# Hybrid attention and RWKV-7 layer on one core: more steps between transfers and their users, follow-ups of dense tiles later, both directions of a scan step together

## The chip, the cores and the metric

The kernel runs on one core of a Trainium2 chip, in float32 throughout. The metric is the device time of one launch in microseconds (us), lower is better. Time is given as the median of the runs; a profiled execution has a time of its own, against which its trace is read.

## The reference, cut to what matters

One layer over 1024 tokens of width 1024. One projection feeds two groups of heads; their outputs are projected back and added to x, then an MLP follows.

```python
h = _rms_norm(x, ln1_g[layer])
proj = h @ w_in[layer]                       # 3*512 columns for q, k, v; 1792 more for u
attn = _dilated_window_attention(q, k, v, q_norm_g[layer], k_norm_g[layer])
rwkv = _rwkv7_bidirectional(u, ...)
x = x + jnp.concatenate([attn, rwkv], axis=-1) @ w_out[layer]
h = _rms_norm(x, ln2_g[layer])
x = x + jnp.square(jax.nn.relu(h @ w_up[layer])) @ w_down[layer]
```

Attention has 8 heads of 64 with normalised queries and keys and three dilated windows, whose results are mixed by their softmax sums. The recurrent group has 8 heads as well. Its state is a 64x64 matrix for each head, carried over the tokens once forwards and once backwards:

```python
def step(state, inp):
    r_t, w_t, k_t, v_t, kk_t, a_t = inp
    s_kk = jnp.einsum('bhvk,bhk->bhv', state, kk_t)
    state = (state * w_t[:, :, None, :]
             - s_kk[..., None] * (kk_t * a_t)[:, :, None, :]
             + v_t[..., None] * k_t[:, :, None, :])
    return state, jnp.einsum('bhvk,bhk->bhv', state, r_t)
```

The outputs of both directions are added, normalised for each head, and a bonus term and a gate follow.

## The kernel before, in words

**Layout and order.** Activations lie transposed, channels on the 128 partitions and tokens along the row, in halves (hf) of 512 tokens. A product of two float32 operands is made from three matmuls of split operands (mm3, lines 104 to 107: high by high, low by high, high by low). The program is written in one order, and a scheduler places the instructions of each engine by readiness and by a priority, which is the place in the program; `ahead(n)` lowers the number for a block, so that it goes n places earlier. An engine then runs its own list strictly in order.

**Stages.** A prologue to 52 us loads x and norms it. `in_proj` (line 164) follows to 603 us, `mixers` (line 839) to 987, and `tail` (line 984), with the output projection and the MLP, to the end.

**in_proj** does two things side by side. The generator `dense` (line 353) makes 26 tiles of 128 projected columns: first the 14 tiles of u, then queries, keys and values (tiles 0 to 11). It yields after every few matmuls. Beside it goes the recurrent preparation of the four head pairs p. `per_half` (line 416) normalises keys and builds decays for one half. `unit_a` (line 447) builds for one half and direction the matrices of 8 chunks of 64 tokens: products psg (L496), masked copies G (L501), and the store gd (L504). Then come transposes psb (L508), their copies BK (L512) and stores to rec_dr. `pair_b` (line 520) inverts 16x16 blocks for both halves of a direction: it loads MP from gd (L524), runs 15 vector steps (stmp L534, Tt L536), stores td and loads the block inverses t16 and t16t. `unit_c` (line 556) then widens them to 64x64 with products psd (L564) and vector steps Nb, Yt, TF (L570, L576, L579). `bonus` (line 582) makes the bonus term. `drive(g, rate)` (line 386) advances such a generator; each of its yields gives the dense work `rate` steps, 0.7, and the pairs waiting in the list `back` 0.6 steps (`behind`). When the units are through, a drain loop gives four dense steps for each step of `back`.

**Follow-ups of dense tiles.** A query or key half is evacuated from PSUM as qc (L322) and squared as qsq (L324). Then, at once, `head_inv` (L124 to L128) takes head sums on TensorE (psq) and their reciprocal rn. `head_rep` widens rn to rx on ScalarE (L133) and turns it by four transposes (L136). The half is scaled (L326), split into qhi (L329) and qlo (L331), and both are stored (L332, L333). A value half is evacuated as vc (L342), turned by four transposes (L345), copied as vn (L348) and stored (L350). qsq, qhi and vn share one buffer (tag qt), and qc, rx and qlo have one each. A second set of these buffers exists from `mixers` on.

**mixers** runs the scan: 16 steps of 64 tokens for each direction d. `load` (line 852) fetches one step's matrices, 1152 KB of rec and four pieces of 64 KB for pv and uv. `step` (line 864) is a chain. It starts with products psc with the state pv (L870), a copy B (L872), and products with B (L874). Two copies follow into uv, one on ScalarE (L875) and one on VectorE (L876). Then come products with uv (L879) and the new state (L882, L883). The outputs psY are made from pv (L886) and uv (L888). The two directions are called one after the other under `ahead(400)`; after each pair `fill(20, 4.7)` gives the remaining dense steps, then pieces of attention under `ahead(200)`. Attention has 64 pieces, 8 for each head, about 12 matmul rows of the built order each: scores ps_s (L701, L702), transposes ps_pt (L719), products with the values pv and pvb (L748). From step 8 on, `post` (line 890) finishes a block of 128 tokens of the recurrent output.

## Time and profile before

| | us |
|---|---|
| runs | 1781.92, 1796.67, 1788.32 |
| median | 1788.32 |
| profiled execution | 1784.77 |
| its span | 1783.0 |
| PE busy in the span | 1649.5 (93%) |
| mean granted clock of TensorE | 0.949 |

Engines are PE (TensorE matmul), PEld (its weight load), DVE (VectorE), ACT (ScalarE), POOL (GpSimd) and SP (SyncE, which issues most DMAs). A row of a timeline is start, duration, engine, line, operation, output<-inputs, and in brackets the idle time ahead of it with what ended it. A row of a table of windows gives for each engine busy time and count, then the granted clock as a share of full speed, the mean busy share of the 16 DMA engines and GB/s. A row of waits is engine, group, what released it, total, number and longest.

### The profile page before, as it was taken

The numbers are of one execution on the slowest core, as the hardware profiler recorded it, in microseconds if no ns is written. First come the engines' busy times: TensorE is split into PE (matmuls) and PEld (weight loads), VectorE is DVE, ScalarE is ACT, GpSimd is POOL, SyncE is SP. The second block draws the span as 40 slices with busy tenths as digits, with TensorE's granted clock in tenths as the row PEclk, the third lists the DMA queues.
The fourth block names the chain that finished last, engine by engine and source line by source line (L and its number), as shares of the span: only waits on it lengthen the run. The fifth ranks groups of instructions, "written<-read, shape, count | busy, mean of one in ns | idle before, by whom it ended". The sixth has DMA issues, their size and how long they took to land. (4 is left out here: it accounts for less than half of the span.)

```text
span 1783.0 us, 29922 instructions
## 1 busy us (share of the span) xinstructions
PE 1649.5 (93%) x11912; PEld 1365.7 (77%) x11912; DVE 861.9 (48%) x1754; ACT 543.5 (30%) x990; POOL 294.2 (16%) x322
## 2 busy tenths in 40 slices
PE   7999978979869997989998999999999999999999
PEld 6777767767757776877786887888888888888887
DVE  6655658757545424565775667332332233223321
ACT  5534334443412213535464234211121112112210
POOL 3022112222200000121223115200120012001200
PEclk9999989879879999988998999999999999999999
DMA  6155788878875599997973411111111111111121
GB/s 221 45 142 125 158 160 174 177 176 176 193 173 135 179 223 202 274 272 210 248 198 108 149 48 54 49 53 48 51 50 47 48 48 48 48 48 54 47 96 53
DMA packets 336923, 223.11 MB, mean 125 GB/s; under 512 B 238320, under 2 KB 289408, under 8 KB 332688
## 3 DMA queue, kind: packets, MB, share of 16 engines
q1 hardware_dynamic: 305520, 195.82, 42.7%
q10 hardware_dynamic: 27680, 15.38, 3.2%
q0 software_dynamic: 3584, 10.00, 2.5%
q8 instruction: 94, 1.54, 0.4%
q14 instruction: 45, 0.37, 0.1%
HBM read 150.22 MB, written 70.91 MB: 124 GB/s over the span
## 5 line engine op out<-in xcount | busy, mean ns | idle before, releaser
L101 ACT CAST w3h<-w3raw 128x512 fp32r<-128x512 f32 (+1 forms) x152 | 90.9, 600 | 397.0 <-PE ps L106 387.3
L106 PE MATMUL ps<-h2l,w3h 128*128 128x512 f32 x512 | 199.2, 389 | 1.1 <-DVE h2l L1045 1.1
L105 PE MATMUL ps<-h2h,w3h 128*128 128x512 f32 x512 | 199.3, 390 | 0.7 <-DVE x L1023 0.7
L107 PE MATMUL ps<-h2h,w3l 128*128 128x512 f32 x512 | 199.2, 389 | 0.0
L1089 POOL TENSOR_TENSOR relu<-relu 128x512 f32<-128x512 f32 x64 | 76.8, 1201 | 530.1 <-DVE relu L1088 530.1
L105 PE MATMUL ps_u<-hh,wh 128*128 128x512 f32 x368 | 156.1, 424 | 3.5 <-DVE ur L308 3.5
L107 PE MATMUL ps_u<-hh,wl 128*128 128x512 f32 x368 | 149.6, 407 | 0.0
L106 PE MATMUL ps_u<-hl,wh 128*128 128x512 f32 x368 | 149.3, 406 | 0.0
L102 DVE TENSOR_TENSOR w3l<-w3raw,w3h 128x512 fp32r<-128x512 f32 (+1 forms) x152 | 105.1, 693 | 79.7 <-ACT w3h L101 79.7
L1097 DVE TENSOR_TENSOR x<-x,ps 128x512 f32<-128x512 f32 x64 | 44.0, 688 | 181.7 <-PE ps L107 181.7
L105 PE MATMUL ps<-rw,w3h 128*128 128x512 f32 x320 | 124.7, 390 | 0.9 <-ACT w3h L101 0.9
L105 PE MATMUL ps<-f,w3h 128*128 128x512 f32 x320 | 124.7, 390 | 0.0
L106 PE MATMUL ps<-rw,w3h 128*128 128x512 f32 x320 | 124.5, 389 | 0.0
L107 PE MATMUL ps<-f,w3l 128*128 128x512 f32 x320 | 124.5, 389 | 0.0
L106 PE MATMUL ps<-f,w3h 128*128 128x512 f32 x320 | 124.5, 389 | 0.0
L107 PE MATMUL ps<-rw,w3l 128*128 128x512 f32 x320 | 124.1, 389 | 0.0
L106 PEld LDWEIGHTS ps<-h2l,w3h 128*128 128x128 f32 x512 | 96.1, 188 | 21.3 <-DVE h2l L1045 1.6
L105 PEld LDWEIGHTS ps<-h2h,w3h 128*128 128x128 f32 x512 | 96.1, 188 | 21.0 <-ACT w3h L101 1.1
L107 PEld LDWEIGHTS ps<-h2h,w3l 128*128 128x128 f32 x512 | 96.1, 188 | 19.9
L1088 DVE SCALAR_TENSOR_TENSOR relu<-ps,rep 128x512 f32<-128x512 f32 x64 | 44.1, 691 | 108.4 <-PE ps L107 108.2
L105 PEld LDWEIGHTS ps_u<-hh,wh 128*128 128x128 f32 x368 | 72.0, 196 | 20.2 <-DVE ur L308 4.3
L106 PEld LDWEIGHTS ps_u<-hl,wh 128*128 128x128 f32 x368 | 71.8, 195 | 16.7 <-issue 2.9
(331 smaller groups left out, 3228.7 us busy)
## 6 DMA issues: line engine op xcount, KB each, us to landing
rec<-rec_dr SPq DMA_DIRECT2D x32, 1152.0 KB, 10.0
w3raw<-in_w_up SPq DMA_DIRECT2D x64, 256.0 KB, 2.5
w3raw<-in_w_dn SPq DMA_DIRECT2D x64, 256.0 KB, 2.5
raw<-in_w_in SPq DMA_DIRECT2D x46, 256.0 KB, 2.9
rec_dr<-al POOLq DMA_DIRECT2D x64, 128.0 KB, 4.2
rec_dr<-G SPq DMA_DIRECT2D x32, 256.0 KB, 4.3
rec_dr<-G SPq DMA_DIRECT2D x64, 128.0 KB, 4.4
rec_dr<-BK ACTq DMA_DIRECT2D x16, 512.0 KB, 5.3
```

Source lines behind the costliest of these rows:

```text
L101: nc.scalar.copy(hi, raw)
L102: nc.vector.tensor_sub(lo, raw, r2f(hi))
L105: nc.tensor.matmul(ps, lh, rh, start=start, stop=False)
L106: nc.tensor.matmul(ps, lh, rl, start=False, stop=False)
L107: nc.tensor.matmul(ps, ll, rh, start=False, stop=stop)
L1088: nc.vector.scalar_tensor_tensor(t, pss[hf], 0.0, rep[:, HS[hf]], ALU.max, ALU.mult)
L1089: nc.gpsimd.tensor_mul(t, t, t)
L1097: nc.vector.tensor_add(x1[c][:, HS[hf]], x1[c][:, HS[hf]], ps)
```

## The change

There are five edits. What the program computes stays the same, and so do the counts of PE, POOL and SP work; 32 copies go from ACT to DVE.

1. **Follow-ups later.** A q, k or v half is evacuated (and squared) as before. What follows is put on a list `late`; a new generator `later` around `dense` advances the first entry by one part after each dense yield, and a query or key follow-up has two parts, cut between rx and its transposes (`head_rep` becomes `head_wide` and `head_turn`). qlo now uses the buffer of rx.
2. **Rates.** `drive` gives 0.62 dense steps a yield and 0.8 steps of `back`; the drain loop gives two dense steps for each of `back`.
3. **More yields** in `per_half` (two), in `pair_b` after the MP load (three for one) and after the loads of t16 (three, or one for the second half); the yield of `bonus` goes ahead of its product.
4. **Preparation products earlier.** psg, psb and psd matmuls go under `ahead(150)`; psg and psb get one tile of two PSUM banks instead of two tiles of one, and psg takes head 1 first.
5. **Scan.** `step` does both directions together, under `ahead(2500)` instead of 400. Heads go 1, 0; both uv copies are on DVE, head 1 last; psY takes the product with uv first, then pv.

```diff
@@ qk_tile
-                    rn = head_inv(sq, 1.0 / HD, NORM_EPS, tq, pq)
...
-                    lo = tq.tile([P, 512], F32R, name="qlo")
...
+                    def rest():
+                        rn = head_inv(sq, 1.0 / HD, NORM_EPS, tq, pq)
+                        rx = head_wide(rn, tq)
+                        yield
+                        nc.vector.scalar_tensor_tensor(qc, qc, qg8 if which == 0 else V("kg"), head_turn(rx, pq), ALU.mult,
+                                                       ALU.mult)
...
+                        lo = tq.tile([P, 512], F32R, name="qlo", tag="rx")
...
+                    late.append(rest())
@@ dense
+            def later():
+
+                for _ in dense():
+                    yield
+                    while late and next(late[0], 1) == 1:
+                        late.pop(0)
+                        break
+                while late:
+                    if next(late[0], 1) == 1:
+                        late.pop(0)
+                    yield
+            filler = later()
@@ drive
-                    behind(0.6)
+                    behind(0.8)
@@ unit_a
-                    pss = [pg.tile([P, 4, P], F32, name="psg") for h in range(2)]
-                    for c in range(4):
-                        for h in range(2):
...
+                    pss = pg.tile([P, 2, 4, P], F32, name="psg")
+                    with ahead(150):
+                        for c in range(4):
+                            for h in (1, 0):
...
@@ pair_b
-                yield
+                for _ in range(3):
+                    yield
...
+                    for _ in range(3 - 2 * hf):
+                        yield
                     yield from unit_c(dict(p=p, d=d, cs=slice(hf * 8, hf * 8 + 8), Ab=Ab, t16=t16, t16t=t16t))
@@ in_proj
-                    drive(per_half(w), 0.7)
+                    drive(per_half(w), 0.62)
...
                 behind(1.0)
-                for _ in range(4):
+                for _ in range(2):
                     next(filler, None)
@@ mixers
-        RH = [(r, h) for r in range(4) for h in range(2)]
+        RH = [(r, h) for r in range(4) for h in (1, 0)]
...
-            nc.scalar.copy(uv[H[0], :, H[0]], ps[H[0], 1])
-            nc.vector.tensor_copy(uv[H[1], :, H[1]], ps[H[1], 1])
...
+            for d in range(2):
+                for h in range(2):
+                    nc.vector.tensor_copy(ws[d]["uv"][H[h], :, H[h]], pss[d][H[h], 1])
...
+                for r in range(4):
+                    for h in (1, 0):
+                        nc.tensor.matmul(psY[H[h], d, r], uv[:, r, H[h]], rec[:, r, h * P + 64:h * P + P],
+                                         start=True, stop=False)
+                    for h in (1, 0):
+                        nc.tensor.matmul(psY[H[h], d, r], pv[:, r, H[h]], rec[:, r, 448 + h * 64:512 + h * 64],
+                                         start=False, stop=True)
...
-            for d in range(2):
-                with ahead(400):
-                    step(d, s, ld[s][d], ld[s + 1][d] if s + 1 < NCH else None, psY[:, d])
+            with ahead(2500):
+                step(s, ld[s], ld[s + 1] if s + 1 < NCH else None, psY)
             fill(20, 4.7)
```

Three places of the built order show what this moves. The first is TensorE in the drain after the last preparation unit, around a query or key half. ps_u are its dense products, psd those of the block inverse, psq at L124 the head sums and at L136 (now L139) the transposes. Before:

```order
L107 MATMUL ps_u<-hh_136,wl 128x512
L564 MATMUL psd<-t16t,Nb 64x64 x16
L124 MATMUL psq<-ct,qsq 128x2 x4
L564 MATMUL psd<-Yt,Nb 64x64 x16
L136 MATMUL psq<-ct,rx 128x128 x4
L105 MATMUL ps_u<-hh_129,wh 128x512
```

The same place now:

```order
L107 MATMUL ps_u<-hh_136,wl 128x512
L601 MATMUL psd<-Yt,Nb 64x64 x8
L124 MATMUL psq<-ct,qsq 128x2 x4
L601 MATMUL psd<-Yt,Nb 64x64 x8
L139 MATMUL psq<-ct,rx 128x128 x4
L601 MATMUL psd<-t_5980,Ab 64x64 x16
L601 MATMUL psd<-t16t,Nb 64x64 x16
L124 MATMUL psq<-ct,qsq 128x2 x4
L105 MATMUL ps_u<-hh_129,wh 128x512
...
L107 MATMUL ps_u<-hh_135,wl 128x512
L139 MATMUL psq<-ct,rx 128x128 x4
L105 MATMUL ps_u<-hh_136,wh 128x512
```

The head sums of a half before now stand within the block's products, and between the head sums and the transposes of the next half there are 21 dense products, where before the next product of the block stood.

The second place is VectorE at the seventh of the eight calls of pair_b, from the last masked product G, after which its store and the load of MP go out, to the first stmp, which uses MP. Before:

```order
L501 TENSOR_TENSOR G<-psg,ct 128x512 x2
L475 TENSOR_TENSOR al<-kkn,EE 128x8x64
L326 SCALAR_TENSOR_TENSOR qc<-qc,qg_111,psq 128x512
L331 TENSOR_TENSOR qlo<-qc,qhi 128x512
L576 TENSOR_TENSOR Yt<-psd,t16t 128x512
L481 SCALAR_TENSOR_TENSOR bk<-tm,Ei 128x8x64
L484 TENSOR_TENSOR bk<-kt,Ei 128x8x64
L591 TENSOR_TENSOR us<-pse,us 128x512
L534 TENSOR_TENSOR stmp<-Tt,MP 128x1
```

Now:

```order
L533 TENSOR_TENSOR G<-psg,ct 128x512 x2
L613 TENSOR_TENSOR Yt<-psd,t16t 128x512
L628 TENSOR_TENSOR us<-pse,us 128x512
L506 TENSOR_TENSOR al<-kkn,EE 128x8x64
L127 TENSOR_SCALAR rn<-psq 128x8
L128 RECIPROCAL rn<-rn 128x8
L616 SCALAR_TENSOR_TENSOR TF<-psd,t16t 128x512
L512 SCALAR_TENSOR_TENSOR bk<-tm,Ei 128x8x64
L515 TENSOR_TENSOR bk<-kt,Ei 128x8x64
L334 SCALAR_TENSOR_TENSOR qc<-qc,qg_111,psq 128x512
L568 TENSOR_TENSOR stmp<-Tt,MP 128x1
```

Nine instructions stand between them now, seven before; the follow-up's last step and the block's are others.

The third place is TensorE at a late scan step. psc and psY are the scan's; ps_s, ps_pt, pvb are attention; psb is the finishing of a block. Before:

```order
L748 MATMUL pvb<-vB,ptsb 128x65 x4
L879 MATMUL psc_10078<-uv_9746,rec_9741 64x64 x8
L888 MATMUL psY<-rec_9741,uv_9746 64x64
L886 MATMUL psY<-rec_9741,pv_9743 64x64 x2
L719 MATMUL ps_pt<-ct,sb 128x128 x4
L124 MATMUL psb__9986<-ct,ysq 128x2 x4
L701 MATMUL ps_s<-kk,qh 128x256
L702 MATMUL ps_s<-kk,ql 128x256
```

Now:

```order
L907 MATMUL psc_9934<-pv_9608,rec_9606 64x64 x8
L124 MATMUL psb__9856<-ct,ysq 128x2 x4
L914 MATMUL psc_9934<-B_9952,rec_9606 64x64 x8
L907 MATMUL psc_9935<-pv_9616,rec_9614 64x64
L139 MATMUL psb__9866<-ct,rx 128x128 x4
L907 MATMUL psc_9935<-pv_9616,rec_9614 64x64 x7
L922 MATMUL psc_9934<-uv_9611,rec_9606 64x64 x8
L930 MATMUL psY<-rec_9606,uv_9611 64x64 x2
L933 MATMUL psY<-rec_9606,pv_9608 64x64 x2
```

Where attention stood between the parts of a step, only the other direction and the finishing of a block stand now. Over the whole order 665 of the 760 matmul rows of attention stood ahead of the last psY before, and 307 now; the first of them came after 6 of the 32 direction steps, and now comes after 10.

More of the change, by code (lines that the diff above doesn't have):

```diff
@@ L200, in in_proj @@
                      [pa[0].tile([P, 512], F32, name="ps_u", tag="acc"), pd.tile([P, 512], F32, name="ps_u", tag="psd")],
-                     [pg.tile([P, 512], F32, name="ps_u", tag="psg") for _ in range(2)]]
+                     pg.tile([P, 2, 512], F32, name="ps_u", tag="psg")]
+            early[2] = [early[2][:, hf] for hf in range(2)]
             with tc.tile_pool(name="xp", bufs=2, side="right", reuse_waits="tile") as xp:
@@ L360, in dense @@
                         yield from qk_tile(c % 4, c // 4)
-                    T.setdefault(c - 12, None)
                     yield
@@ L492, in unit_a @@
                 for g in range(2):
[L493 to L497 removed]
+                    pss = pg.tile([P, 2, 4, P], F32, name="psg")
+                    with ahead(150):
+                        for c in range(4):
+                            for h in (1, 0):
+                                nc.tensor.matmul(pss[:, h, c], bk[H[h], 4 * g + c, h:h + 2].rearrange("p a b -> p (a b)"),
+                                                 al[H[h], 4 * g + c].rearrange("p a b -> p (a b)"), start=True, stop=True)
                     yield
@@ L504, in unit_a @@
                     nc.sync.dma_start(mats(gd, h), Gs[h][H[h], :, 0:64])
-                pss = [pg.tile([P, 8, 64], F32, name="psb", tag="psg") for h in range(2)]
-                for c in range(8):
-                    for h in range(2):
-                        nc.tensor.transpose(pss[h][:, c], bk[H[h], c, h:h + 2].rearrange("p a b -> p (a b)"), K("id2")[H[h]])
+                pss = pg.tile([P, 2, 8, 64], F32, name="psb", tag="psg")
+                with ahead(150):
+                    for c in range(8):
+                        for h in range(2):
+                            nc.tensor.transpose(pss[:, h, c], bk[H[h], c, h:h + 2].rearrange("p a b -> p (a b)"), K("id2")[H[h]])
                 yield
@@ L561, in prod @@
                     ps = v3(pd.tile([P, 512], F32, name="psd"))
-                    for c in range(8):
-                        for h in range(2):
-                            nc.tensor.matmul(ps[H[h], c], L[H[h], c], R[H[h], c], start=True, stop=True)
+                    with ahead(150):
+                        for c in range(8):
+                            for h in range(2):
+                                nc.tensor.matmul(ps[H[h], c], L[H[h], c], R[H[h], c], start=True, stop=True)
                     yield
@@ new lines, in mixers, with step @@
+        RH = [(r, h) for r in range(4) for h in (1, 0)]
+        def step(s, ws, wns, psY):
+            cs = [chunk(d, s) for d in range(2)]
+            pss = [pC.tile([P, 2, 4, 64], F32, name=f"psc{d}") for d in range(2)]
+            for d in range(2):
+                for r, h in RH:
+                    nc.tensor.matmul(pss[d][H[h], 0, r], ws[d]["rec"][:, r, h * P:h * P + 64], ws[d]["pv"][:, r, H[h]],
+                                     start=True, stop=True)
+            Bs = [rt.tile([P, 4, 64], F32, name=f"B{d}") for d in range(2)]
+            for d in range(2):
+                nc.scalar.copy(Bs[d], pss[d][:, 0])
+            for d in range(2):
+                for r, h in RH:
+                    nc.tensor.matmul(pss[d][H[h], 1, r], ws[d]["rec"][H[h], r, 384:448], Bs[d][H[h], r], start=True, stop=True)
+            for d in range(2):
+                for h in range(2):
+                    nc.vector.tensor_copy(ws[d]["uv"][H[h], :, H[h]], pss[d][H[h], 1])
+            for d in range(2):
+                rec, uv, pv = (ws[d][n] for n in ("rec", "uv", "pv"))
+                if wns is not None:
+                    for r, h in RH:
+                        nc.tensor.matmul(pss[d][H[h], 0, r], rec[:, r, 256 + h * 64:320 + h * 64], uv[:, r, H[h]],
+                                         start=True, stop=True)
+                    for h in range(2):
+                        new = wns[d]["pv"][H[h], :, H[h]]
+                        nc.vector.tensor_add(new, pss[d][H[h], 0], pv[H[h], :, H[h]])
+                        nc.vector.tensor_mul(new, new, LC[H[h], d, cs[d]].rearrange("p (r o) -> p r o", o=1).to_broadcast([64, 4, 64]))
+                for r in range(4):
[5 more added lines that the diff above has]
+                                         start=False, stop=True)
```

84 lines of the change are left out of this document (35 added, 49 removed).

## The prediction

> **What bounds the kernel now.** I began with the page: how busy each engine is, and the row of the clock that TensorE was granted.
>
> ```profile
> PE 1649.5 (93%) x11912; PEld 1365.7 (77%) x11912; DVE 861.9 (48%) x1754; ACT 543.5 (30%) x990; POOL 294.2 (16%) x322
> ...
> PEclk9999989879879999988998999999999999999999
> ```
>
> TensorE (PE) is the bound; no other engine reaches half. But its clock dips again and again in the first 1000 us. So I cut the span at the stage borders, which I took from the first and last matmul of each kind: recurrent preparation with dense projections from 52 to 603, scan with attention from 603 to 987, then the output projection and the MLP.
>
> ```profile
> core 0: us, PE busy (x) PEld busy (x) DVE busy (x) ACT busy (x) POOL busy (x), PEclk, DMA share, GB/s
> 52.00:603.00 551.00, 479.80 (x4346) 392.97 (x4344) 337.43 (x675) 203.87 (x316) 100.15 (x173) 0.89 0.68 151
> 603.00:987.00 384.00, 339.04 (x3895) 286.74 (x3896) 208.67 (x618) 161.41 (x392) 67.07 (x41) 0.92 0.84 221
> 987.00:1783.00 796.00, 789.58 (x3499) 652.78 (x3498) 285.54 (x422) 153.09 (x253) 111.24 (x85) 1.00 0.17 56
> ```
>
> The last 796 us are full (6 us idle, clock 1.00) and the change leaves them alone. Everything it can win lies in the first two rows: 551 - 480 = 71 us and 384 - 339 = 45 us of idle PE, and the time lost to a clock of 0.89 and 0.92. Then I read what PE waited for.
>
> ```profile
> PE psq L124 <- ACT qsq L324: 19.6, 11, 9.0
> PE pse L454 <- ACT om L443: 14.7, 3, 7.2
> PE psc L870 <- DMA pv<-vt_dr: 11.5, 4, 5.6
> PE psg L496 <- DVE G L501: 9.0, 7, 4.0
> ...
> PE ps_s L701 <- ACT vn L348: 3.0, 1, 3.0
> ...
> PE psq L136 <- ACT rx L133: 2.3, 4, 1.2
> ...
> PE psq L345 <- ACT vn L348: 1.3, 1, 1.3
> ```
>
> The columns are total, number, longest. The largest wait is a follow-up of a dense tile: the head sums (psq) of a query or key half, which PE meets in its queue right behind the last product of that half. The timeline shows what makes its two long ones.
>
> ```profile
> 499.01 0.16 DVE L534 TENSOR_TENSOR stmp<-Tt,MP 128x1 f32<-128x1 f32 x1 [7.39 <-DMA MP<-gd]
> ...
> 500.67 1.78 PEld L124 LDWEIGHTS psq<-ct,qsq 128*128 128x128 f32 x8 [5.07 <-ACT qsq L324]
> ...
> 527.27 0.63 ACT L324 ACTIVATE qsq<-qc 128x512 f32<-128x512 f32 x1 [9.01 <-DMA kh_dr<-qhi]
> ...
> 527.96 1.86 PE L124 MATMUL psq<-ct,qsq 128*128 128x2 f32 x8 [9.04 <-ACT qsq L324]
> ```
>
> At 499 DVE stood 7.39 us at the first step of a block inverse, for a transfer; the evacuation qc was behind it, the square behind qc, PE behind the square. At 527 the square itself waited for its buffer: qhi of the half before lay in it until its store had landed. The clock follows such waits:
>
> ```profile
> 496.00:509.00 13.00, 8.33 (x84) 7.32 (x86) 9.37 (x34) 1.26 (x2) 0.00 (x0) 0.61 0.53 136
> 509.00:519.20 10.20, 9.06 (x120) 7.04 (x114) 7.24 (x16) 2.83 (x5) 0.00 (x0) 1.00 0.82 161
> 519.20:533.00 13.80, 5.04 (x46) 4.82 (x47) 2.90 (x15) 1.26 (x2) 1.60 (x6) 0.60 0.92 191
> ```
>
> It is 0.61 around the first, 1.00 between, 0.60 around the second.
>
> **Term A, the follow-ups later.** In the built order of before, not one dense product stands between the last product of a query, key or value half and the first matmul of its follow-up, in any of the 24 halves. In the changed order 13 of the 24 have 6 to 24 there, and most of the others two to five products of the block inverse (psd). A dense matmul costs PE what the full last stage shows, 683 / 3001 = 0.228 us, a psd product 1.15 us:
>
> ```profile
> 1100.00:1783.00 683.00, 679.26 (x3001) 562.26 (x2999) 209.94 (x314) 114.58 (x186) 76.31 (x64) 1.00 0.16 52
> ...
> 513.74 1.15 PE L564 MATMUL psd<-Yt,Nb 64*64 64x64 f32 x32 [0.64 <-DVE Yt L576]
> ```
>
> So the cover is 1.4 to 5.5 us, or 2.3 to 5.8, where before it was at most one product in most halves. What the follow-ups cost PE is 19.6 + 2.3 + 3.0 + 1.3 = 26.2 us. The chain they wait for (evacuate, square) is short, so most of it goes; of the 9.04 I keep half, because the store that frees the buffer is now issued later too, and qlo shares the buffer of rx. That leaves 26.2 - 4.5 = 21.7. Against it: the psd products lose the follow-ups that stood between them; at seven places in the drain after 512 two products now follow each other, where before another matmul stood between. One such meeting cost 0.64 (the row above); with the queue of DVE in front of it I take 0.9, 6 us in all. **A = -16.** Bounds: 0 (the buffers hold the loop anyway) and -26.
>
> **Term B, more steps between transfers and users.** On DVE this is not what came out. Between the last masked product G, from which the block's transfer starts, and the first stmp, the eight pairs have 13, 31, 16, 42, 16, 23, 7, 13 instructions before and 11, 22, 12, 30, 8, 19, 9, 20 now: fewer in six, more in the last two, since the units also advance faster (0.8 for 0.6). DVE's three waits there sum to:
>
> ```profile
>   DMA MP<-gd: 28.2, 3
> ```
>
> With 7 in between it waited 7.39 (the row of 499.01), so a pair with 8 or 9 will wait about as long again. I take **B = 0**; bounds +10 (8, 11 and 12 in between wait as well, and A no longer covers it) and -7 (the last two pairs stop waiting). What would stand behind that wait on DVE are qc, G and bk, and PE behind them; A's dense products cover one such wait. The om wait (14.7) and the first psg waits keep their neighbours: nothing.
>
> **Term C, clock.** Without the two long waits the stretches of 0.61 and 0.60 run nearer to 1.00: together 13.0 x 0.39 + 13.8 x 0.40 = 10.6 us of clock, of which the waits themselves (13.9 us) need none. About half is work: **C = -5**; bounds 0 and -10.
>
> [...]
>
> **Term D, the scan ahead of attention.** This is the large move. Both directions now go through one step 2500 priorities ahead. By the built order 665 of 760 attention matmuls stood ahead of the last psY before, now 307. At 12 a piece (64 pieces), that is 56 pieces beside the scan before, 25 now; 39 pieces run with no scan to fill their gaps, instead of 8. First the scan part. It carries nearly all the transfers of the stage:
>
> ```profile
> DMA packets 78922, 84.90 MB, mean 221 GB/s; under 512 B 53487, under 2 KB 67183, under 8 KB 74782
> ...
> rec<-rec_dr SPq DMA_DIRECT2D x32, 1152.0 KB, 10.0
> pv<-vt_dr SPq DMA_DIRECT2D x64, 64.0 KB, 6.2
> uv<-vt_dr SPq DMA_DIRECT2D x64, 64.0 KB, 6.3
> qh<-qh_dr SPq DMA_DIRECT2D x16, 256.0 KB, 6.7
> ...
> x<-in_xT SPq DMA_DIRECT2D x8, 512.0 KB, 4.7
> ...
> 750.00:800.00 50.00, 42.04 (x645) 36.75 (x645) 31.96 (x85) 20.22 (x56) 10.36 (x5) 0.90 1.05 276
> ```
>
> Of the 84.9 MB, the loads of the last three heads (about 2.5 MB each, six of 256 KB like qh, values and bias), xT (4.2) and some 3 of weights and exchanges come after the scan: 70 MB remain. At the 276 GB/s of the stage's best 50 us that is 254 us, at its mean of 221, 317. PE needs less: 32 scan halves, 25 pieces and the rest of the dense work. As the scan's loads no longer wait for attention's steps I take 254. Then the 39 pieces:
>
> ```profile
> 692.00:722.00 30.00, 25.97 (x235) 23.83 (x232) 13.07 (x51) 15.11 (x40) 5.96 (x3) 0.82 1.09 246
> ...
> 953.00:987.00 34.00, 27.97 (x171) 23.86 (x171) 17.00 (x61) 17.33 (x37) 2.54 (x2) 0.80 0.50 176
> 973.50:987.00 13.50, 13.02 (x100) 12.07 (x99) 7.40 (x28) 9.09 (x22) 1.27 (x1) 0.91 0.82 318
> ```
>
> Here attention ran nearly alone. 953 to 987 held 8 pieces and the follow-ups of two last scan blocks: 34 / 8 = 4.25 us a piece. Its last 13.5 us ran 8 pieces' second halves: 1.7. 692 to 722 gave about 3.3. I take 2.6, between the free run and the disturbed one: 101 us. With 8 us for the end: 254 + 101 + 8 = 363, against 384. **D = -21.** Bounds: 254 + 39 x 1.7 + 8 = 328 (-56) and 254 + 39 x 4.25 + 8 = 428 (+44).
>
> **At nothing.** The two copies of uv are both on DVE now:
>
> ```profile
> L876 DVE COPY uv<-psc x32: 427/428/429, 615.7 to 948.5; 64x256 f32<-64x256 f32 x32
> ```
>
> 32 x 0.428 = 13.7 us more on DVE, which stands at 209 of 384 there; in a direction's chain the second copy adds 0.43. The cover is the other direction's psY, (49.5 + 46.3) / 32 = 3.0 us by these rows:
>
> ```profile
> L888 PE MATMUL psY<-rec,uv 128*64 128x64 f32 x512 | 49.5, 240 | 0.5 <-ACT uv L875 0.5
> L886 PE MATMUL psY<-rec,pv 128*64 128x64 f32 x512 | 46.3, 240 | 2.1 <-DVE y L973 1.3 <-ACT y L971 0.8
> ```
>
> Without it, 32 x 0.43 = 14 us. One two-bank psg tile for two one-bank tiles frees both heads at once; its matmuls alternated between the banks before, so both were needed within one step anyway; at worst the 9.0 us of psg waits double.
>
> **Sum.** -16 + 0 - 5 - 21 = -42. The profiled execution took 1784.77 us, of which the span is 1783.0; its stages would give 1741 and 1743. It lies 3.5 us below the median of the three runs shown (1788.32), so for a median I say 1746.
>
> **The rivals.**
> *Attention alone is slow.* With 4.25 us a piece the stage is 428, 44 more than now; with A and C at -21 the whole is 1788 + 23 = 1811. For it: both stretches in which attention ran nearly alone had a clock of 0.82 and 0.80. Against it: the quick end of the second. It breaks even with A and C at (384 + 21 - 262) / 39 = 3.7 us a piece, and is over 1% slower from 4.1. Chance 0.19.
> *The waits only move.* The follow-ups wait for buffers instead (one qt, one rx, each held until a store has landed), DVE stands at MP as before, and the transfers hold the scan at the stage's length: A about -8, the rest nothing, 1780. For it: the 9.01 was such a buffer, and the share of DMA is above 1 in part of the stage. Here also belongs that the change does not do what it says: for B the order already says so. Chance 0.25.
> *Everything fits.* Pieces at 1.7 us, A at its bound: -26 - 10 - 56, cut to what the idle and the clock of the first two stages can give together, about -80: 1708. For it: 116 us of idle there. Against it: the om and MP waits stay. Chance 0.15.
> *The forecast*: 0.41.
>
> **How the numbers follow.** About 1% (18 us) is what a measurement of this kernel can tell from no change. Faster by more: the forecast and the last rival, 0.56, and 0.01 of the second. Slower by more: most of the first, 0.17. Between: 0.26. The forecast's own range is 1722 to 1770, from A between -8 and -22 and a piece between 2.2 and 3.1 us. For 8 in 10 it must take in the second rival, most of the third and the near part of the first: 1695 to 1806.
>
> **What would show it.** Right: PE's waits for qsq under 8 us in total; the last psY before 880 and the first product of the output projection before 970; the clock from 496 to 533 above 0.8. Wrong: a DVE wait for MP over 35 us with PE behind it (B), waits of ACT for a store of qhi above 15 us (second rival), or a stretch from the last psY to the output projection of over 140 us (first rival). If PE's waits go and the time stays, then PE was not the bound there, and the queue of transfers was.

## The result

The changed kernel is slower: a median of 1845.82 us (1841.95 to 1851.38) against 1785.49 for the kernel before beside it, a ratio of 1.0329 with a 95% interval from 1.0272 to 1.0387. The forecast was 1746, its range ended at 1806. The profiled execution took 1841.95 us with a span of 1840.2, 57 more than before.

The page first: the busy row of TensorE and the clock it was granted.

```profile
PE 1643.5 (89%) x11912; PEld 1368.4 (74%) x11912; DVE 877.0 (48%) x1786; ACT 533.1 (29%) x958; POOL 292.2 (16%) x322
...
PEclk9998988888879899799877899999999999999999
```

TensorE does the same 11912 matmuls in nearly the same busy time (1643.5 us, 1649.5 before); it stands idle more. The stages, cut again at the first and last matmul of each kind (the last two rows divide the second stage at the scan's last output):

```profile
core 0: us, PE busy (x) PEld busy (x) DVE busy (x) ACT busy (x) POOL busy (x), PEclk, DMA share, GB/s
51.00:643.00 592.00, 489.84 (x4380) 397.95 (x4380) 346.97 (x680) 207.81 (x322) 97.25 (x174) 0.87 0.64 142
643.00:1041.00 398.00, 320.95 (x3831) 282.29 (x3832) 215.24 (x642) 145.36 (x349) 67.56 (x40) 0.85 0.82 211
1041.00:1840.00 799.00, 792.78 (x3528) 655.98 (x3525) 284.20 (x426) 154.81 (x258) 110.71 (x85) 1.00 0.18 56
643.00:914.00 271.00, 222.98 (x3202) 191.91 (x3202) 153.53 (x421) 81.32 (x196) 31.91 (x22) 0.89 1.01 255
914.00:1041.00 127.00, 97.97 (x632) 90.38 (x631) 61.71 (x221) 64.04 (x153) 35.65 (x18) 0.77 0.40 117
```

The preparation takes 592 us for 551, scan and attention 398 for 384, the tail 799 for 796. In the preparation TensorE is busy 10 us longer and idle 31 us more. In the second stage it is busy 18 us less and idle 32 us more, at a clock of 0.85 for 0.92.

What TensorE now waits for, and two of ScalarE's waits:

```profile
PE psd L601 <- DMA t<-td: 20.3, 5, 8.5
PE psd L601 <- DVE Yt L613: 18.8, 5, 8.3
...
PE psq L124 <- ACT qsq L328: 7.4, 4, 3.3
PE psd L601 <- DVE Tt L570: 6.5, 1, 6.5
PE psd L601 <- DVE Nb L607: 6.3, 4, 2.2
```

```profile
ACT qsq L328 <- DMA kh_dr<-qhi: 26.7, 5, 11.4
...
ACT qsq L328 <- DMA qh_dr<-qhi: 23.8, 6, 7.7
```

The rows before that belong beside them, the largest wait at psd and ScalarE's wait for a store of qhi:

```profile
PE psd L564 <- DVE Yt L576: 4.3, 4, 1.7
```

```profile
ACT qsq L324 <- DMA kh_dr<-qhi: 9.4, 2, 9.0
```

The wait for the square, 19.6 us before, is down to 7.4, as forecast. In its place TensorE stands 20.3 + 18.8 + 6.5 + 6.3 = 51.9 us at the products of the block inverse, where before all its waits at psd came to 11.3. Ahead of the square ScalarE stands 26.7 + 23.8 = 50.5 us for the stores of qhi, 9.4 before.

The drain shows how this comes about. These rows are one turn of it in the changed kernel, in order of time:

```profile
592.50 0.68 PE L601 MATMUL psd<-t,Ab 64*64 64x64 f32 x16
...
594.64 0.62 ACT L337 CAST qhi<-qc 128x512 fp32r<-128x512 f32 x1 [1.64 <-DVE qc L334]
...
598.73 0.63 ACT L328 ACTIVATE qsq<-qc 128x512 f32<-128x512 f32 x1 [3.47 <-DMA kh_dr<-qhi]
598.95 0.69 DVE L613 TENSOR_TENSOR Yt<-psd,t16t 128x512 f32<-128x512 f32 x1 [1.65 <-PE psd L601]
...
602.56 0.63 PE L105 MATMUL ps_u<-hh,wh 128*128 128x512 f32 x1
...
606.31 0.39 PE L105 MATMUL ps_u<-hh,wh 128*128 128x512 f32 x1
...
607.67 0.60 PE L139 MATMUL psq<-ct,rx 128*128 128x128 f32 x4
608.37 0.75 DVE L334 SCALAR_TENSOR_TENSOR qc<-qc,vt,psq 128x512 f32<-128x512 f32 x1 [6.66 <-PE psq L139]
...
610.60 0.69 DVE L326 TENSOR_TENSOR qc<-ps_u,acc 128x512 f32<-128x512 f32 x1
...
614.34 0.68 PE L601 MATMUL psd<-Yt,Nb 64*64 64x64 f32 x16
...
617.75 1.15 PE L601 MATMUL psd<-t,Ab 64*64 64x64 f32 x32
```

The transposes at 607.67 stand behind 21 dense products. Until then qc, the one buffer for an evacuated half, is held; the next half is evacuated at 610.60, right after the follow-up has let go of it. Meanwhile 48 dense products run in one clump, parted only by the transposes, and Yt, ready at 599.64, waits until 614.34 for its product. One turn, from a first product of the inverse (t,Ab) to the next, holds 48 dense products and four of the inverse and takes 617.75 - 592.50 = 25.3 us. Before, the same 48 and four came around in 584.58 - 564.76 = 19.8:

```profile
564.76 1.15 PE L564 MATMUL psd<-t,Ab 64*64 64x64 f32 x32
...
584.58 1.15 PE L564 MATMUL psd<-t,Ab 64*64 64x64 f32 x32
```

The clock makes about 1.8 of these 5.5 us: from 601.13, behind the waits, nine dense products start 0.43 us apart (granted clock 0.53), and from 604.95 on 0.23 (1.00). The rest, 3.6, lies between the dense products: in the waits and slow products of an inverse that nothing covers (from 592.50 to 601.13 TensorE is idle for 2.3 us at a clock of 0.81, and the 32 products at 597.36 take 1.55 us for 1.15).

The drain as a whole, first before, then in the changed kernel:

```profile
506.50:603.00 96.50, 83.14 (x904) 68.51 (x904) 48.89 (x109) 20.02 (x33) 1.60 (x6) 0.92 0.57 135
```

```profile
523.00:643.00 120.00, 99.39 (x906) 81.70 (x906) 52.38 (x117) 22.92 (x38) 1.69 (x7) 0.82 0.45 111
```

The number of matmuls is the same, 904 and 906; 23.5 us are lost, with the clock at 0.82 for 0.92. Another 16.5 are lost ahead of the drain (472 us from 51 on, 455.5 before), of which the follow-ups alone make 4 (below); what makes the rest is open.

### The profile page after: what moved, and what is told of

It is laid out like the page before. It is cut to its first block, busy times and chain, and to the rows that moved or that the text cites. A ratio compares the mean times of both kernels' runs of the same rounds, so it can differ in the third digit from the quotient of the medians.

```text
span 1840.2 us, 29939 instructions
## 1 busy us (share of the span) xinstructions
PE 1643.5 (89%) x11912; PEld 1368.4 (74%) x11912; DVE 877.0 (48%) x1786; ACT 533.1 (29%) x958; POOL 292.2 (16%) x322
## 5 line engine op out<-in xcount | busy, mean ns | idle before, releaser
L106 PE MATMUL ps_u<-hl,wh 128*128 128x512 f32 x368 | 155.2, 422 | 0.0
L107 PE MATMUL ps_u<-hh,wl 128*128 128x512 f32 x368 | 154.7, 420 | 0.0
L105 PEld LDWEIGHTS ps<-h2h,w3h 128*128 128x128 f32 x512 | 96.1, 188 | 20.9 <-ACT w3h L101 1.1
L1133 DVE SCALAR_TENSOR_TENSOR relu<-ps,rep 128x512 f32<-128x512 f32 x64 | 44.1, 691 | 108.5 <-PE ps L107 108.4
```

Of the source, the lines that this page charges most:

```text
L105: nc.tensor.matmul(ps, lh, rh, start=start, stop=False)
L106: nc.tensor.matmul(ps, lh, rl, start=False, stop=False)
L107: nc.tensor.matmul(ps, ll, rh, start=False, stop=stop)
L1133: nc.vector.scalar_tensor_tensor(t, pss[hf], 0.0, rep[:, HS[hf]], ALU.max, ALU.mult)
```

## The experiments

Each ratio is to runs of the kernel before on the same chip, whose medians were 1785 to 1793 us.

| kernel | median us | ratio | 95% interval |
|---|---|---|---|
| before + scan edit | 1817.41 | 1.0152 | 1.0096 to 1.0208 |
| before + follow-ups later | 1820.41 | 1.0165 | 1.0091 to 1.0239 |
| before + yields | 1812.88 | 1.0131 | 1.0095 to 1.0168 |
| before + rates | 1806.82 | 1.0095 | 1.0060 to 1.0130 |
| before + products earlier | 1802.66 | 1.0076 | 1.0048 to 1.0105 |
| yields, rates, products earlier together | 1808.42 | 1.0116 | 1.0079 to 1.0154 |
| all five: the changed kernel | 1845.82 | 1.0329 | 1.0272 to 1.0387 |

### The first set: which part

**The changed kernel, products of the inverse back in their place.**

```diff
-                    with ahead(150):
-                        for c in range(8):
+                    for c in range(8):
```

> The changed kernel with its products of the block inverse (psd) back at their own place in the order: ahead(150) is taken from them alone. Theory P (the products stand too early, so TensorE stands at psd for td, Yt, Tt and Nb: 52 us of such waits in the changed profile, 6.5 before): the preparation from 51 to 643 loses some 30 us, 1845 becomes about 1812, and those waits fall under 20 us. Theory F (the follow-ups in single buffers clump the dense products, 48 in a row, and the inverse loses its cover): no change beyond 10 us, 1835 to 1850. Theory R (the rates give too little dense work): no change either.

It gave 1856.69 us, 1.0389 (1.0338 to 1.0440). Nothing comes back, and the time lies over every theory's range, F's by 7 us. TensorE's waits at psd shrink to 32 us, but the head sums wait 20.9 us for the square instead: the wait changes its place and the time stays. One more thing moved: 55 dense products are left to the scan stage here (counted in the trace behind the last product of the inverse), 144 in the changed kernel. At the price that the run with the yields alone shows below, 26 us for 168, the other 89 cost some 14 us (an estimate), and a gain of 30 would have shown beside that. The first theory falls.

**The changed kernel with the old rates.**

```diff
-                    behind(0.8)
+                    behind(0.6)
...
-                    drive(per_half(w), 0.62)
+                    drive(per_half(w), 0.7)
...
-                for _ in range(2):
+                for _ in range(4):
                     next(filler, None)
```

> The changed kernel with the old rates: 0.7 dense steps and 0.6 steps of the waiting pairs a yield, and four dense steps for each step in the drain. Theory R (half the dense work beside each step of the drain leaves the inverse uncovered; the drain took 119.7 us after, 96.5 before): about 1820, with the drain near 100. Theory P: within 10 us of 1845, since the products still stand too early. Theory F: within 10 us or slower, since the built order now has 37 of 63 gaps between products of the inverse without a dense product, where the changed kernel has 30.

It gave 1852.42 us, 1.0357 (1.0312 to 1.0401). The old rates do not bring the time back. What they are worth by themselves this does not say, because no dense product is left to the scan stage here, where the changed kernel leaves 144 and the kernel before 168. Of the three theories F, the follow-ups, was left as the one to test.

**The scan edit alone, on the kernel before.**

```diff
-            for d in range(2):
-                with ahead(400):
-                    step(d, s, ld[s][d], ld[s + 1][d] if s + 1 < NCH else None, psY[:, d])
+            with ahead(2500):
+                step(s, ld[s], ld[s + 1] if s + 1 < NCH else None, psY)
```

`step` itself is the new one of the diff above. The copies of psY at the end of a step, which also stood under `ahead(400)`, go under 2500 with it.

> The kernel before with the scan edit alone: both directions in one step, 2500 ahead, uv on VectorE, heads 1, 0. Theory A (attention left alone is slow: 127 us after the last output of the scan at a clock of 0.77): the stage from 603 grows by 15 to 20 us, 1785 becomes about 1803. Rival: the scan edit gains or costs nothing by itself, and what the stage lost came from the dense work that the preparation left to it: 1775 to 1790.

It gave 1817.41 us: 27 to 30 slower, more than theory A had. The stage divides so, first until the scan's last output, then until the output projection:

```profile
603.00:894.70 291.70, 244.85 (x3282) 208.39 (x3276) 155.73 (x437) 93.22 (x213) 31.87 (x23) 0.87 0.95 240
894.70:1015.50 120.80, 89.48 (x609) 81.60 (x607) 56.52 (x213) 59.78 (x147) 36.90 (x18) 0.80 0.43 124
```

The scan part, with its transfers at a share of 0.95, ends 58 us earlier than before (894.7 for 953.0). What attention has left then runs 121 us with TensorE idle for 31 of them and at a clock of 0.80, where before the last part took 35 (953.0 to 988.2).

**The follow-ups later alone, on the kernel before.**

```diff
+                    def rest():
+                        rn = head_inv(sq, 1.0 / HD, NORM_EPS, tq, pq)
+                        rx = head_wide(rn, tq)
+                        yield
...
+                    late.append(rest())
...
-            filler = dense()
+            filler = later()
```

> The kernel before with the follow-ups later alone (qlo in the buffer of rx included). Theory F (they clump the dense products, so that two products of the inverse follow each other without cover, 28 of 63 gaps now and 22 before): 10 to 30 us slower, 1795 to 1815, with waits of TensorE at psd above 25 us. Theory P and Theory R: as the prediction had it, up to 16 us faster, 1769 to 1785.

It gave 1820.41 us, 29 to 33 slower: theory F has the size, although this kernel keeps the old rates and the old place of the products. Waits at psd came to 14.3 us for td and 13.5 for Yt. The drain took 126 us (510.8 to 636.9), 30 more than before with 35 more dense products in it (8 us); ahead of it only 4 were lost. Two turns of it, 96 dense products and eight of the inverse, take 54.1 us, 27 each for the 19.8 of before:

```profile
558.05 1.22 PE L592 MATMUL psd<-t,Ab 64*64 64x64 f32 x32 [0.21 <-DVE TF L607]
...
612.17 1.22 PE L592 MATMUL psd<-t,Ab 64*64 64x64 f32 x32 [0.79 <-DVE TF L607]
```

### The second set: why

**The new scan step under the old ahead(400).**

```diff
-            with ahead(2500):
+            with ahead(400):
                 step(s, ld[s], ld[s + 1] if s + 1 < NCH else None, psY)
```

> The kernel before with the new scan step (both directions together, uv on VectorE, heads 1, 0, psY with uv first), but under ahead(400) as before. Theory A (it is the place, 2500 ahead, which takes attention out from between the scan's steps and leaves it alone): within 12 us of before, 1776 to 1800. Theory S (the new step itself is the cost: longer chains on VectorE, both directions stalled by one transfer): near the scan edit alone, 1805 to 1820.

It gave 1794.57 us, 1.0023 (1.0003 to 1.0042). The step itself, with both uv copies on VectorE, costs next to nothing.

```profile
602.00:935.00 333.00, 292.13 (x3579) 247.81 (x3580) 183.34 (x536) 121.89 (x288) 53.08 (x33) 0.88 0.91 232
935.00:989.70 54.70, 44.16 (x291) 40.39 (x291) 32.31 (x114) 31.60 (x73) 15.91 (x9) 0.81 0.44 143
```

Set beside the run with 2500: moving the scan further ahead ends it 40.3 us earlier (935.0 to 894.7) and makes the rest 66.1 us longer (54.7 to 120.8). The 318 matmuls that moved (609 - 291) cost 40 us beside the scan and 66 alone.

**The old step under ahead(2500).**

```diff
-                with ahead(400):
+                with ahead(2500):
                     step(d, s, ld[s][d], ld[s + 1][d] if s + 1 < NCH else None, psY[:, d])
```

> The kernel before with its own scan step, one direction after the other, but under ahead(2500). Theory A: near the scan edit alone, 1805 to 1820, with 110 us or more from the last psY to the output projection. Theory S: within 12 us of before.

It gave 1806.32 us, 1.0083 (1.0054 to 1.0112), with 117 us from the last psY to the output projection. So the place alone makes about half of the scan edit's loss, the step alone hardly any. Place and step together come to 0.5% more than their sum, which these intervals do not tell from nothing.

**Follow-ups later, from the second yield on.**

```diff
+                old = 0
                 for _ in dense():
                     yield
-                    while late and next(late[0], 1) == 1:
-                        late.pop(0)
-                        break
+                    if old:
+                        while late and next(late[0], 1) == 1:
+                            late.pop(0)
+                            break
+                    old = len(late)
```

> Follow-ups later alone, and a follow-up is first advanced at the second yield after it was listed, not the first. The first yield after the second half of a tile comes with no product behind it: there the built order had 0 dense products between the half and its head sums, and the two halves of a tile ran as 48 products in one clump. Now 23 of the 24 halves have 6 to 24. Theory F1 (the clump and the uncovered second half are the cost): back to 1775 to 1795. Theory F2 (the single buffers qc, qt and rx hold the loop whatever the order): stays at 1805 to 1830.

It gave 1819.05 us, 1.0155 (1.0111 to 1.0199), the same as the follow-ups alone and in the range of F2. But this does not make F1 fall, because a second thing moved here too: the run before it leaves 144 dense products to the scan stage, this one none, and dense work taken out of that stage cost time by itself (26 us for 168 products in the run with the yields alone, below). In the drain the mended order did help. Two turns, again 96 dense products, take 44.1 us, 22 each for 27:

```profile
549.21 1.15 PE L595 MATMUL psd<-t,Ab 64*64 64x64 f32 x32
...
593.27 1.15 PE L595 MATMUL psd<-t,Ab 64*64 64x64 f32 x32
```

So the clump is a part of the cost. The buffer is not out of it either; ScalarE still stood at the store:

```profile
ACT qsq L327 <- DMA qh_dr<-qhi: 25.6, 6, 7.3
...
ACT qsq L327 <- DMA kh_dr<-qhi: 7.4, 3, 3.1
```

**The same with two buffers for qsq, qhi and vn.**

```diff
-                    sq = tq.tile([P, 512], F32, name="qsq", tag="qt")
+                    sq = tq.tile([P, 512], F32, name="qsq", tag="qt", bufs=2)
...
-                        hi = tq.tile([P, 512], F32R, name="qhi", tag="qt")
+                        hi = tq.tile([P, 512], F32R, name="qhi", tag="qt", bufs=2)
```

> The same, and the buffer of qsq, qhi and vn (tag qt) doubled, so that a square need not wait for the store of the half before. Theory F1: no better than with one buffer, 1775 to 1795. Theory F2: clearly faster than with one buffer, by 15 us or more, and ScalarE's waits of qsq for the stores of qhi are gone.

It gave 1802.54 us, 1.0063 (1.0035 to 1.0091): 16.5 us faster than with one buffer, and ScalarE's waits for qhi's stores are gone. Two turns of the drain take 38.0 us, 19 each:

```profile
551.95 1.15 PE L595 MATMUL psd<-t,Ab 64*64 64x64 f32 x32
...
589.92 0.79 PE L595 MATMUL psd<-t,Ab 64*64 64x64 f32 x18
```

So the turn that had grown from 19.8 to 27 us is back at about its old length: 5 us came back with the order, 3 with the buffer, which had been held until its store had landed. The 16.5 us are not all from there. In the profiled executions the preparation ends 4 us earlier than with one buffer (641.7 for 645.8), but the stage with scan and attention is 17 us shorter (360.5 for 377.7), and why is not shown. This kernel too leaves no dense product to that stage; at 26 us for 168 that alone would account for the 10 us by which it is slower than before. Long waits remain at the next such buffer, rx, which now also holds qlo (12.8 and 9.2 us at the longest):

```profile
ACT rx L133 <- DMA ql_dr<-qlo: 12.8, 1, 12.8
```

```profile
PE psq L139 <- ACT rx L133: 11.9, 5, 9.2
```

A second buffer for rx or qc was not tried.

### The third set: what else costs

**The changed kernel without follow-ups and scan edit.** What remains are the rates, the yields and the earlier products.

```diff
-                    late.append(rest())
...
-            filler = later()
+            filler = dense()
...
-            with ahead(2500):
+                with ahead(400):
```

> The changed kernel without its two large edits: follow-ups at once and the old scan step under ahead(400); what remains are the rates, the yields, the earlier preparation products and the two-bank psg tile. If the costs of the follow-ups (about 30 us) and of the scan (about 30 us) simply add up to the 60 measured, this is within 10 us of before, 1780 to 1800. If the remaining edits cost something that the follow-ups hid: above 1800. If they pay and the two large edits cost more together than apart: under 1778.

It gave 1808.42 us, 1.0116 (1.0079 to 1.0154). What the prediction had held at nothing is 17 to 21 us by itself. With 30 for the follow-ups and 30 for the scan that is more than the 60 measured, though not by more than the intervals leave open.

**The kernel before with two buffers for qsq, qhi and vn.**

```diff
-                    sq = tq.tile([P, 512], F32, name="qsq", tag="qt")
+                    sq = tq.tile([P, 512], F32, name="qsq", tag="qt", bufs=2)
...
-                    lo = tq.tile([P, 512], F32R, name="qlo")
+                    lo = tq.tile([P, 512], F32R, name="qlo", tag="rx")
```

> The kernel before with two buffers for qsq, qhi and vn; qlo goes into the buffer of rx to make room, nothing is moved later. Theory F2 (the one buffer, held until a store has landed, is what TensorE waited for): the wait of 9 us at the head sums goes, 5 to 12 us faster, 1776 to 1784. Rival (the wait moves to the next buffer, rx with qlo in it, or to the block inverse): no change within 4 us.

It gave 1788.59 us, 0.9980 (0.9962 to 0.9997). The longest wait at the head sums, 9 us, is gone, and a wait of nearly the same length stands at the next product of the inverse ("issue" is a wait for nothing that the profile shows):

```profile
PE psd L564 <- issue: 8.7, 1, 8.7
...
PE psq L124 <- ACT qsq L324: 4.3, 10, 0.8
```

The total at the head sums fell from 19.6 to 4.3 us, the time by 3. The product that now waits starts at 531.33 us, and at 529.75 before; those right behind it wait 0.58 us for td, so the wait for the square had most likely covered one for that transfer. The rival was right: the wait moved.

**Follow-ups later, second yield, two buffers, and two dense steps in the drain.** The edit is the count of the drain loop, 4 to 2.

> Follow-ups later, advanced from the second yield on, two buffers for qsq, qhi and vn, as in the fourth run of the second set, and the drain gives two dense steps instead of four, so that 72 dense products (16 us of TensorE) are left to the scan stage where none were. Theory G (dense work beside the scan is nearly free, because the transfers set that stage's length, so taking it into the preparation is what kept that run 10 us above before): 10 to 16 us faster than that run's 1802, about 1790. Rival: the inverse loses that cover in the drain and nothing is won, 1797 to 1810.

It gave 1796.46 us, 1.0038 (1.0013 to 1.0063), 6 us less than with four steps. That lies between the two expectations and decides little.

### The fourth set: the three small edits, each alone

**The yields.**

```diff
...
-                yield
+                for _ in range(3):
+                    yield
...
+                    for _ in range(3 - 2 * hf):
+                        yield
                     yield from unit_c(dict(p=p, d=d, cs=slice(hf * 8, hf * 8 + 8), Ab=Ab, t16=t16, t16t=t16t))
```

> The kernel before with the extra yields alone (two in the unit of a half, two more after the MP load, three or one after the loads of t16, the moved one in the bonus). Each yield hands dense work out at the old rate, so the built order leaves no dense product to the scan stage, where before 168 were left (38 us of TensorE). Theory G (dense work is nearly free beside the scan, and costs its time in the preparation): 10 to 20 us slower, 1800 to 1810. Rival: the yields give transfers the time they are meant to and nothing is lost, 1780 to 1795.

It gave 1812.88 us, 1.0131 (1.0095 to 1.0168). The two stages:

```profile
51.00:651.00 600.00, 551.19 (x4572) 452.41 (x4571) 349.94 (x694) 216.87 (x333) 98.13 (x179) 0.89 0.65 144
651.00:1013.00 362.00, 301.74 (x3657) 260.99 (x3654) 191.88 (x598) 155.98 (x376) 67.11 (x35) 0.83 0.81 214
```

No dense product is left to the scan stage. With the 168 that were, 38 us of TensorE, the preparation is 48 us longer (600 for 552 from 51 on) and the second stage 22 shorter (362 for 384), a loss of 26 for the two. Theory G has that: a dense product cost less beside the scan, where TensorE had gaps (45 us of 384 idle before), than in the preparation. What the yields do besides is in these numbers too.

**The products earlier.**

```diff
+            pg = s1.enter_context(tc.tile_pool(name="pg", bufs=1, side="right", space=PSUM, reuse_waits="tile"))
...
+                    with ahead(150):
...
```

> The kernel before with the earlier preparation products alone: psg, psb and psd under ahead(150), one psg tile of two banks, head 1 first. Theory P, in what is left of it (TensorE meets these products before VectorE has made their operands; 28 of 63 gaps between products of the inverse hold no dense product, before 22): 8 to 16 us slower, 1796 to 1806, with waits at psd of 15 us or more. Rival (the yields or the rates carry the cost): within 5 us of before.

It gave 1802.66 us, 1.0076 (1.0048 to 1.0105), with TensorE standing 18.7 us at psd for Yt and td, as theory P had both.

```profile
PE psd L568 <- DVE Yt L580: 13.7, 2, 9.1
...
PE psd L568 <- DMA t<-td: 5.0, 3, 3.8
```

**The rates.** The edit is the reverse of that of the second run in the first set.

> The kernel before with the rates alone: 0.62 and 0.8 for 0.7 and 0.6, and two dense steps in the drain for four. The built order hardly changes where the dense work stands (144 products left to the scan, before 168). All theories: within 8 us of before, 1782 to 1798; a larger loss would say that the waiting pairs, run faster, meet their transfers earlier than these land.

It gave 1806.82 us, 1.0095 (1.0060 to 1.0130). All theories had less. The preparation ends 3 us earlier than before (599.7), and VectorE waits 19.7 us for MP (28.2 before), so the pairs do not meet their transfers too early; the loss is in the stage with scan and attention (406 us for 384), and it goes with the clock (0.82 over that stage for 0.92). Its cause stays open.

**Two buffers and two dense steps in the drain, on the kernel before.**

```diff
-                    sq = tq.tile([P, 512], F32, name="qsq", tag="qt")
+                    sq = tq.tile([P, 512], F32, name="qsq", tag="qt", bufs=2)
...
-                for _ in range(4):
+                for _ in range(2):
                     next(filler, None)
```

> The kernel before with two buffers for qsq, qhi and vn (as in the third set) and two dense steps in the drain, which leaves 192 dense products to the scan for 168. Theory G: 24 products, 5 us, cost nothing beside the scan; 1783 to 1788, the fastest of all. Rival (the drain loses cover): 1790 or more.

It gave 1777.35 us, 0.9941 (0.9916 to 0.9967): the fastest of all, 0.6% under the kernel before. The stretch from 700 to the scan's last output, first with the rates alone, then in this kernel:

```profile
700.00:926.80 226.80, 199.31 (x2306) 171.16 (x2302) 128.03 (x403) 101.37 (x243) 47.23 (x25) 0.80 0.86 220
```

```profile
700.00:907.50 207.50, 190.50 (x2403) 164.10 (x2400) 128.05 (x405) 97.68 (x247) 45.38 (x24) 0.91 0.95 250
```

Here 97 matmuls more are done in 19 us less, at a clock of 0.91 for 0.80. The two kernels differ in the rates and in the buffer.

### The fifth set: buffer or drain

**Two dense steps in the drain alone, on the kernel before.** The edit is the count of the drain loop, 4 to 2.

> The kernel before with two dense steps for four in the drain and nothing else: 192 dense products are left to the scan stage, 168 before. If the work left to the scan made the gain: 1776 to 1783. If it takes both (the second buffer lets the drain run with less cover): within 4 us of before.

It gave 1787.49 us, 1.0011 (0.9999 to 1.0024). So it takes both, the second buffer and the drain; the buffer alone gave 0.9980, the two 0.9941.

**Two buffers and one dense step in the drain.** The count is 1 for 2.

> Two buffers for qsq, qhi and vn as before, and one dense step in the drain for two. Theory G: equal or a little faster than 1777. Rival: the inverse loses its cover, and the time is 1785 or more.

It gave 1807.29 us, 1.0122 (1.0088 to 1.0156), as the rival had it. It does not test theory G as meant: the trace has 168 dense products behind the last product of the inverse, where the run with two steps has 192: fewer, not more. One step in a loop count makes 30 us, 1777 to 1807. In the profiled executions the preparation ends within 1 us in both (597.9 and 596.9); from there to the first product of the output projection it is 373 and 398 us. What in the new placement does this is open.

## Why the prediction was wrong, step by step

**Where the time goes.** Right: it is all in the first two stages, the tail is as it was.

**Term A, -16, was the step that failed first; it has the wrong sign.** Alone the follow-ups cost about 30 us. The prediction counted the dense products that come to stand behind a half as cover and took 0 as the worst. It saw that the 9.01 us wait was a buffer and kept half of one wait for that. It did not ask what the move makes of a turn of the drain. In the order of before, a half's follow-up ran at once and its last steps lay under the next half's 24 products. Moved later, it lets the dense work come in clumps of 48 with the block inverse uncovered between them, and it holds its buffers until its stores have landed, while the next square is due. A turn went from 19.8 us to 27 by that; the mended order brought it to 22, the second buffer to 19. Two of the prediction's own signs of being right came true all the same: the wait for the square shrank from 19.6 to 7.4 us (under 8 was the sign), and the clock from 496 to 533 was 0.82 (above 0.8). The sum of a wait is thus no bound for a move that changes who waits. Against the term stood 6 us for products of the inverse that follow each other; with the follow-ups alone TensorE's waits at psd are 31 us, for 11 before.

**Term B and "at nothing".** The row it rested on came out as forecast: VectorE's wait for MP is 26.5 us in six pieces, 28.2 in three before. (One more wait at the same step is put down to Tt, 10.6 us, 4.6 before; with it the sum is 37.1 for 32.8.)

```profile
DVE stmp L568 <- DMA MP<-gd: 26.5, 6, 13.3
```

The term still failed, since this wait was not all that the yields and rates do. A yield hands out dense work, and the prediction priced neither that nor ahead(150) on the products of the inverse. Alone, yields, rates and earlier products cost 1.3%, 0.95% and 0.8%; together 1.2%.

**Term C, -5.** Wrong with A: the clock rose in the stretch that it was read from (496 to 533, 0.71 to 0.82) and fell over the stages as a whole, 0.89 to 0.87 and 0.92 to 0.85. In the turn above the slow products behind the waits cost about 1.8 us.

**Term D, -21.** Its mechanism was seen, its sizes were off. The scan part needs 271 us, not 254: the transfers ran at a share of 1.01, but at a mean of 255 GB/s, not at the 276 of the best 50 us.

```profile
DMA packets 66692, 69.23 MB, mean 255 GB/s; under 512 B 49248, under 2 KB 58592, under 8 KB 62560
```

The bytes, 69 MB of the 70 assumed, were right. Attention alone took 128 us (914.0 to 1042.3); less the 8 for the end that is 3.2 us for each of the 38 pieces (453 matmul rows by 12), not 2.6. Together 17 and 19 us, which turns -21 into +15, and the stage grew by 14. Alone, the scan edit cost 27 to 30; the changed kernel leaves 24 dense products less to this stage, 5 us.

**The rivals.** "Attention alone is slow" names the second half of what happened, with 4.25 us a piece for the 3.2 measured; its break-even at 3.7 took A and C as gains of 21. "The waits only move" names the first half: ScalarE's waits for the stores of qhi, over 15 us as its sign, are 50.5. The first rival's own sign, over 140 us from the last psY to the output projection, did not come (128). Each was priced as if the other did not hold, and the second as a gain of 8 us. Part of each came true, at once, which no case in the prediction allowed.

**The range** ended at 1806 because A and C stood as gains in the case that set its upper end. With A at the 30 us that it costs alone, D at +15 and the small edits at nothing, the same sum is 1788 + 45 = 1833. No term is left for the rest, about 15 us; the small edits cost 17 to 21 alone.

**What stays open:** why the five edits cost 6.2% when taken alone and added, and 3.3% together (the three small ones 3.0% and 1.2%); what was lost ahead of the drain; why a second buffer of the preparation shortens the scan stage; and what goes with a clock between 0.80 and 0.91 there for orders that differ little.

## What to carry to other kernels

Before moving a follow-up later, list the buffers it holds and what is queued for them, and look in the built order at what then stands between the products of the other chain. Here later was a longer hold and a clump rather than cover, and its bound belonged on the side of a loss. Work that filled TensorE's gaps beside the scan, where the DMA share was 0.91, was cheap only there: taken out, it was left to be paid alone (66 us for what had cost 40), and other filler work, put in the earlier, fuller stage, cost more than its own time (48 us for 38). So count, before reading a total, how much filler work each order leaves to which stage: here it came to 168, 144, 120, 55 or 0 in runs whose edit was about something else, and one of them would have refuted theory F1 by its total alone. In an order made by a scheduler, price every edit that hands out work, the yields too, and take a spread of some tens of microseconds as given for edits that look neutral.

## What the runs showed of the chip

Attention alone ran slowly in three kernels in which the scan's last output left it 79 us or more: the changed kernel (127 us), the scan edit alone (121) and the rates alone (79). There it was granted a clock of 0.77, 0.80 and 0.76 and used TensorE for 77, 74 and 76% of the time, at a DMA share of 0.40, 0.43 and 0.45. In the changed kernel TensorE's longest waits there are for ScalarE (9.7, 4.9 and 4.6 us in total), and the profile puts none down to a transfer. In a turn of the changed kernel's drain waits were seen to cost twice, once as idle time (2.3 us) and again as slow matmuls behind them (0.43 us apart at a clock of 0.53, for 0.23 at 1.00). In the scan stage, clock and length moved together (0.80 and 0.91 over some 200 us, with 19 us between them and 97 matmuls more on the shorter side); which of the two makes the other is not shown.
